# Moving the on-chip tiles of a hybrid encoder block so that their rows begin at multiples of 2 KB

## The chip, the core and the metric

The kernel runs on one core of a Trainium2 chip. The metric is device time in microseconds (us): the median of several executions. One more execution was recorded by the hardware profiler; its span is the time from the first to the last instruction of the program, and the execution's own time is a little longer than that.

The engines are TensorE (PE in the profile; PEld is its loading of the stationary operand), VectorE (DVE), ScalarE (ACT), GpSimd (POOL) and SyncE (SP). The on-chip memory has 128 partitions; a tile occupies the same byte range in each of them, and the tile's *offset* in this document is where that range begins. A matmul of this kernel reads two operands from it: the stationary one (128 columns of 4 bytes, 512 bytes per partition) and the moving one (256, 384 or 512 columns of 4 bytes).

## What is computed

One layer of an encoder block on 512 tokens of width 1024, all in float32:

```
xn   = rms_norm(h, g_mix);  proj = xn @ w_in          # 1024 -> 2048
h    = h + concat(short_conv(proj), pool(proj)) @ w_o # 1024 -> 1024
xn   = rms_norm(h, g_ffn);  q = xn @ w_q              # 1024 -> 2048
s    = q . sub_keys          # 8 heads x 2 halves x 128 keys
top-16 of each half -> 256 candidates -> top-16 experts of 16384, softmax
h    = h + sum_k gate_k * gelu(u_k . xn) * v_k
gate = sigmoid(rms_norm(h, g_ple) @ w_ple_gate)       # 1024 -> 1024
out  = rms_norm(h + gate * (p @ w_ple_proj), g_final)
```

## The kernel before

Every float32 product is made from three matmuls: an operand x is split into a high part H, which ScalarE writes as a copy in the reduced float32 format, and a low part L = x - H, which VectorE writes; then the kernel sums H·H, H·L and L·H (`mm3`, `mm3_pair`; lines 123, 125 and 127). A row of the profile such as `o<-vH,wL` names the output, then the moving operand, then the stationary one.

The stages follow each other along the span:

1. **Input projection** (from about 18 us): eight pieces of `w_in`, 256 columns each. `projT` multiplies a piece (stationary, `wH`/`wL`) with the transposed activations (moving, 512 columns, `xH`/`xL`). A piece is 48 matmuls.
2. **Output projection** (until about 160 us): the mixed activations `mixH`/`mixL` are stationary, the pieces of `w_o` (`wH`/`wL`, 256 columns) move.
3. **Query projection** (about 169 to 280 us): again `projT`, eight pieces of `w_q`; after each, 16 small matmuls with the keys give the scores, and VectorE begins the top-16 searches.
4. **First expert phase** (until about 640 us): for three of the four token groups, 384 tokens, all experts are evaluated densely, in blocks of 128. For each of the first 76 blocks `score` makes 24 matmuls: block `uH`/`uL` stationary, `xH`/`xL` moving with 384 columns. The blocks come by DMA into two buffers `uraw`; a load is issued when VectorE has made `uL` from the block before in that buffer. VectorE works through the top-16 searches meanwhile, and `onehot` spreads the gates with fp16 matmuls. The fourth token group gathers its experts row by row with indirect DMAs into `gr`.
5. **Second expert phase** (until about 1397 us): `mix` multiplies a block of `expert_v` (`vH`/`vL`, moving, 512 columns) with the weighted activations (`wH`/`wL` of the pool `wq`, stationary) into six accumulators `o`; the remaining 52 `score` blocks run in between, into `u`.
6. **Tail**: for each of the four token groups `tail_gate` multiplies the transposed activations `tH`/`tL` (stationary) with the gate weights. These lie in tiles that are free by then (`xH`/`xL` for the left 512 columns; `uraw`, `uH`, `uL` for the right 512) and move. The last group does its right half in two parts of 256 columns.

Memory is handed out by pools that grow from two ends. Pools without a side grow from the low end: the constants, then `xH`/`xL`, the `u` blocks, and in the second phase the `v` blocks and the pool `wq`. Pools with `side="right"` grow down from the high end: first `h`, then the weight pieces, `mixH`/`mixL`, scores, later `gr`, `gres`, the one-hot tiles and the tail's `tH`/`tL`. Tiles of a later stage take the place of those of an earlier one in the same stack.

The order of the instructions of the first four stages comes from a scheduler that runs when the program is built; the second expert phase and the tail stand in the order of the code.

Of the kernel before, what the change touches and what calls it, by code (L numbers as in the profile page):

```python
# [7 lines left out]
F32 = mybir.dt.float32  # L8
# [8 lines left out]
P = 128  # L17
# [43 lines left out]
def block_kernel(ctx: ExitStack, tc: tile.TileContext, x, pT_in, g_cols, w_in, conv_w, pool_w,  # L61
# [4 lines left out]
    consts = ctx.enter_context(tc.tile_pool(name="consts", bufs=1))  # L66
    dram = ctx.enter_context(tc.tile_pool(name="dram", bufs=1, space=bass.MemoryType.DRAM))
    small = ctx.enter_context(tc.tile_pool(name="small", bufs=2))
    sbx = ExitStack()
    xpool = sbx.enter_context(tc.tile_pool(name="xt", bufs=1))  # L70
    sh = ExitStack()
# [19 lines left out]
    eidx = consts.tile([P, P], I32, name="eidx")  # L91
    gate3 = consts.tile([P, P], F32, name="gate3")
    xrow = consts.tile([P, D], F32, name="xrow")

    def split_ld(src, hi, lo):
        nc.scalar.activation(hi, src, AF.Copy)
        nc.vector.tensor_tensor(lo, src, hi.bitcast(F32), op=OP.subtract)
# [900 lines left out]
```

## Time and profile before

| | before |
|---|---|
| median of 3 runs (lowest to highest) | 1455.18 us (1454.88 to 1456.47) |
| profiled execution, its own time | 1454.46 us |
| its span | 1452.7 us |
| mean granted TensorE clock | 0.994 of full speed |
| matmuls recorded | 7785 |

The profiled execution lies 0.72 us under the median and 1.8 us over its own span. TensorE's share of busy time in such a profile counts from the start of a matmul to its end, and matmuls overlap, so it shows whether TensorE waits and not how fast it goes; how fast it goes is the step from the start of one matmul to the start of the next, which the timeline gives.

### The profile page before, as it was taken

The page shows a single profiled execution, that of the slowest core. Times are in us where ns is not written, and L with a number is a line of the kernel's source. Part 1 is how long each engine was busy: PE and PEld are TensorE (multiplying, and loading weights), DVE is VectorE, ACT ScalarE, POOL GpSimd, SP SyncE. Part 2 cuts the span into 40 slices and gives each one's busy share as a digit, 9 for nine tenths or more (in the row PEclk, how much of TensorE's full clock was granted, in tenths as well). Part 3 has the DMA queues.
Part 4 walks back from the last instruction along what each step waited for, and adds up shares of the span by engine and source line. Part 5 has one row for each costly group of instructions (what it writes and reads, how often), then busy time and mean ns, then how long its engine had stood idle before and what let it go on. Part 6 is the DMA issues. An engine that isn't in the chain of part 4 may idle for free.

```text
span 1452.7 us, 20601 instructions
## 1 busy us (share of the span) xinstructions
PE 1430.8 (98%) x7785; PEld 1271.6 (88%) x7785; DVE 1137.7 (78%) x2078; ACT 614.5 (42%) x864; POOL 390.7 (27%) x260
## 2 busy tenths in 40 slices
PE   8999999999998999999999999999999999999997
PEld 5789888999998999998999999999998888788886
DVE  5644579899998987879988778888877777776765
ACT  5321533344564665664333333333333334433354
POOL 0000000002132132125766555454443123342000
PEclk9999999999998999999999999999999999999999
DMA  8223730047688899899998999998997899998721
GB/s 302 87 90 104 242 116 30 30 164 279 227 285 268 274 316 326 262 317 347 380 349 323 375 329 339 347 339 324 346 336 273 317 334 333 335 342 324 249 70 73
DMA packets 152083, 381.38 MB, mean 263 GB/s; under 512 B 10928, under 2 KB 72112, under 8 KB 151728
## 3 DMA queue, kind: packets, MB, share of 16 engines
q1 hardware_dynamic: 72400, 211.75, 41.3%
q0 software_dynamic: 36864, 134.23, 25.3%
q10 hardware_dynamic: 42720, 34.08, 7.2%
q8 instruction: 61, 1.00, 0.3%
q14 instruction: 38, 0.31, 0.1%
HBM read 339.92 MB, written 40.11 MB: 262 GB/s over the span
## 4 chain that ended last, share of the span: by engine, by line
PE 71%; DVE 12%; DMA 7%; issue 6%; ACT 2%; POOL 1%; ACTq 1%; SPq 0%; DVEq 0%; POOLq 0%
PE o L127 11%; PE o L123 11%; PE o L125 11%; PE acc L125 6%; PE acc L123 6%; PE acc L127 6%; PE u L127 5%; PE u L123 5%; PE u L125 5%; DMA uraw<-in_u_blk 3%; DVE uL L586 2%; DMA tH<-in_w_gate 2%; POOL gr L536 1%; PE acc L191 1%; PE tp L516 1%
## 5 line engine op out<-in xcount | busy, mean ns | idle before, releaser
L536 POOL DMA_INDIRECT gr<-in_u_rows,eidx x128 | 201.1, 1571 | 652.5 <-DVE tsm L390 334.6
L536 POOL DMA_INDIRECT gr<-in_v_rows,eidx x128 | 189.4, 1480 | 285.2 <-DVE xrow L560 274.5
L125 PE MATMUL o<-vL,wH 128*128 128x512 f32 x768 | 237.2, 390 | 0.7 <-DVE vL L604 0.7
L123 PE MATMUL o<-vH,wH 128*128 128x512 f32 x768 | 237.7, 390 | 0.3 <-ACT wH L685 0.3
L127 PE MATMUL o<-vH,wL 128*128 128x512 f32 x768 | 237.3, 390 | 0.1
L598 ACT ACTIVATE vH<-vraw 128x1024 fp32r<-128x1024 f32 x128 | 135.4, 1058 | 218.3 <-PE o L127 160.8
L123 PE MATMUL acc<-xH,uH 128*128 128x384 f32 x608 | 206.6, 340 | 3.4 <-ACT uH L580 3.4
L604 DVE TENSOR_TENSOR vL<-vraw,vH 128x1024 fp32r<-128x1024 f32 x128 | 156.2, 1221 | 65.2 <-ACT vH L598 64.9
L125 PE MATMUL acc<-xL,uH 128*128 128x384 f32 x608 | 206.8, 340 | 0.0
L127 PE MATMUL acc<-xH,uL 128*128 128x384 f32 x608 | 204.7, 339 | 0.2 <-DVE uL L586 0.2
L580 ACT ACTIVATE uH<-uraw 128x1024 fp32r<-128x1024 f32 x128 | 135.3, 1058 | 100.6 <-DMA uraw<-in_u_blk 64.0
L586 DVE TENSOR_TENSOR uL<-uraw,uH 128x1024 fp32r<-128x1024 f32 x128 | 155.7, 1217 | 24.8 <-ACT uH L580 24.8
L125 PEld LDWEIGHTS o<-vL,wH 128*128 128x128 f32 x768 | 144.0, 188 | 32.3 <-DVE vL L604 1.5
L127 PEld LDWEIGHTS o<-vH,wL 128*128 128x128 f32 x768 | 143.9, 188 | 31.2 <-DVE wL L690 1.0
L560 DVE SCALAR_TENSOR_TENSOR xrow<-gr,gate,xrow 128x1024 f32<-128x1024 f32 x128 | 164.1, 1282 | 5.1 <-DMA xrow<-h_d 4.6
L123 PEld LDWEIGHTS o<-vH,wH 128*128 128x128 f32 x768 | 143.3, 188 | 27.2 <-ACT wH L685 0.7
L556 DVE SCALAR_TENSOR_TENSOR gr<-gr,xrow 128x1024 f32<-128x1024 f32 x128 | 154.3, 1218 | 4.2 <-DMA gr<-in_u_rows,eidx 4.1
L127 PE MATMUL u<-xH,uL 128*128 128x384 f32 x416 | 139.6, 336 | 0.0
L123 PE MATMUL u<-xH,uH 128*128 128x384 f32 x416 | 139.5, 335 | 0.0
L125 PE MATMUL u<-xL,uH 128*128 128x384 f32 x416 | 139.3, 335 | 0.0
L123 PEld LDWEIGHTS acc<-xH,uH 128*128 128x128 f32 x608 | 115.4, 190 | 4.1 <-ACT uH L580 4.1
L127 PEld LDWEIGHTS acc<-xH,uL 128*128 128x128 f32 x608 | 115.1, 189 | 0.8 <-DVE uL L586 0.8
(214 smaller groups left out, 2336.8 us busy)
## 6 DMA issues: line engine op xcount, KB each, us to landing
uraw<-in_u_blk SPq DMA_DIRECT2D x128, 512.0 KB, 5.2
vraw<-in_v_rows SPq DMA_DIRECT2D x128, 512.0 KB, 6.0
G_d<-stage ACTq DMA_DIRECT2D x12, 1664.0 KB, 12.8
gq<-G_d SPq DMA_DIRECT2D x26, 768.0 KB, 7.0
A_d<-a ACTq DMA_DIRECT2D x17, 768.0 KB, 6.0
aq<-A_d SPq DMA_DIRECT2D x17, 768.0 KB, 9.5
wraw<-in_w_in SPq DMA_DIRECT2D x8, 1024.0 KB, 5.8
wraw<-in_w_q SPq DMA_DIRECT2D x8, 1024.0 KB, 5.8
```

Of the source, the lines that this page charges most:

```text
L123: nc.tensor.matmul(ps, lh, rh, start=start, stop=False)
L125: nc.tensor.matmul(ps, lh, rl, start=False, stop=False)
L127: nc.tensor.matmul(ps, ll, rh, start=False, stop=stop)
L191: nc.tensor.matmul(ps, pT[:, c, t * P:(t + 1) * P], wp[hf][:, c], start=c == 0, stop=c == 1)
L516: nc.tensor.matmul(ps[:, o:o + P], qb[b][:, t * P:(t + 1) * P], keys[:, 2 * hd + b], start=True, stop=True)
L536: nc.gpsimd.indirect_dma_start(out=g, out_offset=None, in_=table, in_offset=bass.IndirectOffsetOnAxis(ap=eidx[:, k:k + 1], axis=0))
L556: ins = nc.vector.scalar_tensor_tensor(g, g, 1.0, xrow, op0=OP.mult, op1=OP.mult, accum_out=act[:, k:k + 1])
L560: ins = nc.vector.scalar_tensor_tensor(accg, g, gate3[:, k - P:k - P + 1], accg, op0=OP.mult, op1=OP.add)
L580: nc.scalar.activation(ublk[i][1], ublk[i][0], AF.Copy)
L586: nc.vector.tensor_tensor(ublk[i][2], raw, uh.bitcast(F32), op=OP.subtract)
L598: nc.scalar.activation(vblk[n][1], vblk[n][0], AF.Copy)
L604: nc.vector.tensor_tensor(vblk[n][2], raw, vh.bitcast(F32), op=OP.subtract)
```

## The change

Two tiles are added that nothing reads or writes: 2016 bytes per partition as the first tile of the right side, and 256 bytes after the constants of the left side that are allocated first.

```diff
     small = ctx.enter_context(tc.tile_pool(name="small", bufs=2))
+    right = ctx.enter_context(tc.tile_pool(name="right", bufs=1, side="right"))
+    right.tile([P, 504], F32, name="rpad")
     sbx = ExitStack()
...
     xrow = consts.tile([P, D], F32, name="xrow")
+    consts.tile([P, 64], F32, name="lpad")
```

In the built program the offsets of the tiles move as follows (bytes per partition; in brackets the remainders by 2048 and by 64). Other buffers of a name lie whole multiples of 512 bytes further on.

| tile | side | before | with the change |
|---|---|---|---|
| `xH`, `xL` | left | 16128, 32512 (1792, 0) | 16384, 32768 (0, 0) |
| `uraw`, `uH`, `uL` | left | 48896, 57088, 69376 (1792, 0) | 49152, 57344, 69632 (0, 0) |
| `vH`, `vL` | left | 93952, 106240 (1792, 0) | 94208, 106496 (0, 0) |
| `wH`, `wL` of the second phase | left | 130816, 136960 (1792, 0) | 131072, 137216 (0, 0) |
| `wH`, `wL` of the projections | right | 180192, 196576 (2016, 32) | 178176, 194560 (0, 0) |
| `mixH`, `mixL` | right | 114656, 131040 (2016, 32) | 112640, 129024 (0, 0) |
| `tH`, `tL` of the tail | right | 176096, 184288 (2016, 32) | 174080, 182272 (0, 0) |
| `gr` | right | 204768 (2016, 32) | 202752 (0, 0) |
| `stage`, `a4` | right | 128992, 155616 (2016, 32) | 126976, 153600 (0, 0) |

No instruction is added, removed or moved on any engine. Only what three instructions of VectorE wait for changes, since other old and new tiles now share bytes: each of the `uL` below may only be written when the stores of `pleo` that lay there have landed. The first rows are VectorE's before, at the end of the transposition that precedes the query projection; the names in brackets are the semaphores waited for, where `DMAHW` stands for a DMA.

```order
153 L586 TENSOR_TENSOR uL<-uraw,uH 128x1024 [waits DMAHW4_49,Activation_49]
154 L139 SCALAR_TENSOR_TENSOR xL<-g,gcol,xH 128x512 [waits Activation_49]
155 L139 SCALAR_TENSOR_TENSOR xL<-tp,gcol,xH 128x512 [waits Activation_49]
156 L335 TENSOR_TENSOR xrow<-xs 128x1024 [waits DMAHW6_49,DVE_49]
157 L586 TENSOR_TENSOR uL<-uraw,uH 128x1024 [waits DMAHW3_49,DMAHW5_49,DMAHW2_49,Activation_49]
158 L586 TENSOR_TENSOR uL<-uraw,uH 128x1024 [waits DMAHW7_49,Activation_49]
159 L97 TENSOR_TENSOR wL<-wraw,wH 128x2048 [waits DMAHW1_49,PE_49,Activation_49]
160 L348 MAX tv<-s 128x8 [waits DMAHW0_49,Activation_49]
```

The same place with the change (line numbers are three higher there):

```order
153 L589 TENSOR_TENSOR uL<-uraw,uH 128x1024 [waits DMAHW7_49,DMAHW4_49,Activation_49]
154 L142 SCALAR_TENSOR_TENSOR xL<-g,gcol,xH 128x512 [waits Activation_49]
155 L142 SCALAR_TENSOR_TENSOR xL<-tp,gcol,xH 128x512 [waits Activation_49]
156 L338 TENSOR_TENSOR xrow<-xs 128x1024 [waits DMAHW6_49,DVE_49]
157 L589 TENSOR_TENSOR uL<-uraw,uH 128x1024 [waits DMAHW2_49,DMAHW5_49,DMAHW0_49,Activation_49]
158 L589 TENSOR_TENSOR uL<-uraw,uH 128x1024 [waits DMAHW7_49,DMAHW3_49,Activation_49]
159 L100 TENSOR_TENSOR wL<-wraw,wH 128x2048 [waits DMAHW1_49,PE_49,Activation_49]
160 L351 MAX tv<-s 128x8 [waits Activation_49]
```

The first, second and third `uL` wait for the first, the second and third, and the fourth of the last four `pleo` stores (line 193); before, it was the second `uL` (third and fourth store) and the `MAX` behind (second store). The instructions stand where they stood.

## Rows read from the trace of the kernel before

**Rows 1.** The page: the span, and busy us (share of the span) and instructions by engine.

```profile
span 1452.7 us, 20601 instructions
...
PE 1430.8 (98%) x7785; PEld 1271.6 (88%) x7785; DVE 1137.7 (78%) x2078; ACT 614.5 (42%) x864; POOL 390.7 (27%) x260
```

**Rows 2.** Groups by shape: line, engine, out<-in, shape, count | busy us, mean ns.

```profile
L123 PE MATMUL o<-vH,wH 128*128 128x512 f32 x768 | 237.7, 390 | 0.3 <-ACT wH L685 0.3
L123 PE MATMUL acc<-xH,uH 128*128 128x384 f32 x608 | 206.6, 340 | 3.4 <-ACT uH L580 3.4
L123 PE MATMUL u<-xH,uH 128*128 128x384 f32 x416 | 139.5, 335 | 0.0
L123 PE MATMUL acc<-xH,wH 128*128 128x512 f32 x256 | 83.3, 401 | 0.5 <-ACT xH L138 0.5
L123 PE MATMUL o<-xH,tH 128*128 128x512 f32 x32 | 12.9, 403 | 0.0
```

**Rows 3.** Timeline of PE, input projection: start us, us, instruction, count.

```profile
100.07 0.63 PE L123 MATMUL acc<-xH,wH 128*128 128x512 f32 x2
...
102.87 0.63 PE L123 MATMUL acc<-xH,wH 128*128 128x512 f32 x2
```

**Rows 4.** Timeline of PE, second expert phase, `mix`.

```profile
1289.91 0.62 PE L123 MATMUL o<-vH,wH 128*128 128x512 f32 x2
...
1295.35 0.62 PE L123 MATMUL o<-vH,wH 128*128 128x512 f32 x2
```

**Rows 5.** Timeline of PE, second expert phase, `score`.

```profile
702.79 0.33 PE L123 MATMUL u<-xH,uH 128*128 128x384 f32 x1
...
704.87 0.33 PE L123 MATMUL u<-xH,uH 128*128 128x384 f32 x1
```

**Rows 6.** Timeline of PE, output projection.

```profile
129.91 0.28 PE L123 MATMUL acc<-wH,mixH 128*128 128x256 f32 x1
...
131.47 0.28 PE L125 MATMUL acc<-wL,mixH 128*128 128x256 f32 x1
```

**Rows 7.** Timeline of PE, tail, last token group.

```profile
1438.95 0.28 PE L123 MATMUL o<-uraw,tH 128*128 128x256 f32 x1
...
1441.05 0.28 PE L123 MATMUL o<-uH,tH 128*128 128x256 f32 x1
```

**Rows 8.** DMA queues (packets, MB, share of 16 engines) over the whole span.

```profile
q1 hardware_dynamic: 72400, 211.75, 41.3%
q0 software_dynamic: 36864, 134.23, 25.3%
```

**Rows 9.** The longest of PE's waits between 40 and 640 us: total us, times, longest.

```profile
PE acc L123 <- ACT uH L580: 3.4, 3, 2.6
```

**Rows 10.** Windows: busy us and count by engine, PEclk, DMA share, GB/s.

```profile
190.00:240.00 50.00, 50.00 (x250) 41.56 (x249) 44.88 (x250) 16.34 (x20) 0.00 (x0) 1.00 0.28 85
240.00:280.00 40.00, 40.00 (x214) 34.51 (x213) 32.98 (x210) 10.11 (x16) 0.00 (x0) 1.00 0.00 1
280.00:440.00 160.00, 159.42 (x1031) 156.85 (x1031) 157.00 (x527) 85.42 (x128) 31.11 (x19) 1.00 0.68 229
450.00:460.00 10.00, 9.31 (x47) 8.87 (x48) 8.27 (x9) 5.06 (x11) 1.35 (x2) 0.66 1.03 329
460.00:470.00 10.00, 8.52 (x60) 7.67 (x59) 6.17 (x8) 6.06 (x11) 1.06 (x2) 0.85 0.56 189
```

**Rows 11.** Waits of VectorE between 190 and 280 us.

```profile
DVE tv L348 <- ACT s L518: 12.4, 5, 5.4
```

**Rows 12.** Timeline of ACT around 450 us; in brackets the idle time before and what ended it.

```profile
449.24 1.06 ACT L580 ACTIVATE uH<-uraw 128x1024 fp32r<-128x1024 f32 x1 [2.36 <-DMA uraw<-in_u_blk]
```

**Rows 13.** The stores of `pleo` (line 193): issues, first and last start; landing.

```profile
L193 SPq DMA_DIRECT2D ple_d<-pleo x8: 319/320/357, 13.8 to 168.7; - x8
...
DMA to landing us min/median/max: 5.8/7.2/8.4
```

**Rows 14.** Timeline of DVE: the first `uL`.

```profile
176.74 1.23 DVE L586 TENSOR_TENSOR uL<-uraw,uH 128x1024 fp32r<-128x1024 f32 x1 [0.99 <-ACT uH L580]
```

## The prediction

> **What bounds the kernel now.** I read the page first: TensorE is busy for 1430.8 of 1452.7 us [rows 1]. That says that it hardly waits, not that it is fast, since overlapping matmuls make "busy" blind to the distance between them. PE's waits come next: between 40 and 640 us, where DMA and VectorE are most in its way, the longest kind comes to 3.4 us in three times [rows 9]. So almost everywhere the time is the number of matmuls times the step from one start to the next, and the question is whether a tile's offset enters that step.
>
> The groups by shape raise the question by themselves. Matmuls of 512 columns last 390 ns on average in `mix`, but 401 in the projections and 403 in the tail [rows 2]. The timeline gives the steps; in each of these stretches PE runs without a wait:
>
> - `mix`, 512 columns: 24 matmuls from 1289.91 to 1295.35 us, 226.7 ns each [rows 4].
> - `score`, 384 columns: 12 from 702.79 to 704.87, 173.3 ns [rows 5].
> - Output projection, 256 columns: 13 from 129.91 to 131.47, 120.0 ns [rows 6].
> - Input projection, 512 columns: 12 from 100.07 to 102.87, 233.3 ns [rows 3].
> - Tail, 256 columns: 18 from 1438.95 to 1441.05, 116.7 ns [rows 7].
>
> From 384 to 512 columns (`score`, `mix`) the step grows by 53.4 ns, 0.417 ns a column, which is one column a cycle at the upper clock level of 2.4 GHz. Take 0.417 ns a column off each, and there remain 13.3 ns in `mix`, `score` and the output projection, 20.0 in the input projection and 10.0 in the tail's 256 columns. Two families, then. The table of offsets separates them: in the first three both operands lie on the same side, so their remainders by 64 are equal (0 and 0, or 32 and 32); in the last two the stationary operand lies on the right (32) and the moving one on the left (0). The strongest pair is output projection and tail: both take 256 columns, both run the same `mm3` chain into one bank, and their steps differ (120.0 and 116.7). Between them hardly anything but the operands' places is different.
>
> **What the change does, part by part.** No instruction moves; the pads cost no time.
>
> *Same-side matmuls* (`score`, `mix`, output projection): both operands move by the same number of bytes, so what they are to each other stays. The absolute remainder by 2048 does change, from 1792 or 2016 to 0. Does a moving row that crosses a multiple of 2 KB cost anything? In the output projection the moving rows of 1024 bytes begin at remainders 2016 and 992 in turn, so every second chunk of three matmuls crosses one and the next does not, and all 13 steps sum to 120.0 each [rows 6]. The stationary slices of `uH`, 512 bytes from remainder 1792 on, cross one in every fourth chunk; 12 steps over four chunks stay at 173.3 [rows 5]. So I take nothing here. The bound on the gain side is what exceeds 0.417 ns a column: 13.3 ns on 768 x 3 matmuls of `mix` and (608 + 416) x 3 of `score` [rows 2], 71 us. The bound on the loss side is that they fall into the slow family: 6.7 ns on 2304 of `mix`, 15 us.
>
> *Right-against-left matmuls* (both projections of 512 columns, the tail): afterwards both operands have remainder 0, as `mix` and `score` have now. If the remainder by 64 is what sorts the families, the step falls from 233.3 to 226.7. Their number is 256 x 3 = 768 `projT` matmuls [rows 2], of which half belong to each projection, and in the tail 32 x 3 = 96 for the left half [rows 2] plus three groups' right halves at 24 each, 168 together. 936 x 6.67 ns = 6.2 us. The last group's right half, 48 matmuls of 256 columns, would go the other way, from 116.7 to 120.0: 0.2 us lost. Sum: 6.1 us gained. From below: zero, if the offset isn't the reason.
>
> Does the gain reach the end? The first 2.6 us (input projection) do: PE paces that stage and all behind it shifts. The second 2.6 us (query projection) must also be taken up by VectorE, which has the top-16 searches there and is busy for 44.88 of 50 us from 190 to 240 and 157.00 of 160 from 280 to 440 [rows 10]. But from 240 to 280 it is busy for only 32.98 of 40 [rows 10], and in all it waits 12.4 us for the scores that PE feeds [rows 11]. It has caught up by then, so scores that come 2.6 us earlier let it go on earlier. If I am wrong there, these 2.6 us come back as waits of PE for `uL`, and the sum is 3.5 us. The tail's 0.9 us lies on the path to the last output.
>
> *DMA.* The gathers write to `gr`, remainder 32 by 64; most of the other loads write to `uraw` and `vraw`, remainder 0. Per engine the first queue moves 134.23 MB in 25.3% of 16 x 1452.7 us, 22.8 GB/s; the other 211.75 MB in 41.3%, 22.1 GB/s [rows 8]. The offset that is less round is not slower, so I take nothing. The bound for a gain is what PE loses around 450 us to a late load of `uraw`: 2.6 us of wait [rows 9, 12], and after it a granted clock of 0.66 over 10 us and 0.85 over the next [rows 10], about 9.8 us at the lower level, 1.2 GHz, worth 4.9 us: 7.5 us.
>
> *The three waits of VectorE.* The last `pleo` store is issued at 168.7 us and stores land within 8.4 us, by 177.1 [rows 13]; the first `uL` begins at 176.74 [rows 14] and waits for the first of the four, not the last. Nothing, then; without that cover, at most 0.4 us.
>
> Sum against the profiled execution: 1454.46 - 6.1 = 1448.4 us. The median lies 0.72 us above that execution, so the forecast for it is 1449.1 us.
>
> **A rule that speaks against this.** The Trainium skill, "TensorE: Matmul & The Clock Gate", section "Step-by-step: what each phase is for", says that PE reads the moving operand and the stationary one through two independent ports, so that loading the next tile's weights takes nothing from the running matmul. By that rule no offset of one to the other could matter, and the change would give 1455.2 us; the mechanism of the first rival below is this one. The same page's section "Back-to-back issue gap" gives N/2.4 + 2.5 ns for one matmul, 215.8 ns at 512 columns as an estimate; the trace agrees with neither family, at 226.7 and 233.3 [rows 3, 4].
>
> **The rivals.**
>
> *No change.* The families come from something that only coincides with the sides, such as the order in which stationary operands alternate: `projT` changes it with every matmul, `mix` keeps it for two. For it: five stretches are few. Against it: `score`, output projection and tail share one order of operands and fall into both families [rows 5 to 7]. Time: the median of before, 1455.2, give or take 1.2.
>
> *Half of it is swallowed.* The query projection's 2.6 us end at VectorE, as above: 1451.7 us.
>
> *Slower.* The place is the first expert phase around 450 us. There a `uraw` load is issued when VectorE is done with its predecessor, and PE already waited 2.6 us for one [rows 9, 12] and then fell to the lower clock [rows 10]. If PE comes 5.1 us earlier and neither VectorE nor the loads do, the 5.1 us turn into further waits, of which each of some 2.6 us brings a fall of the clock like the first one (0.66 over 10 us: 6.8 us at half speed, 3.4 us lost). Two more falls: 1455.2 - 6.1 + 5.1 + 6.8 = 1461.0. It decides from the point where waits and clock give back more than 9 us. Against it: VectorE waits for PE before this phase [rows 11], so both come earlier together.
>
> *More than forecast.* Rounder offsets make DMA quicker, the late load around 450 us is in time, and 7.5 us come on top: 1441.6. The rates of the two queues speak against it [rows 8]. The Trainium skill, "DMA: Bandwidth & Descriptors", section "How a descriptor splits into AXI transactions", has such a rule for reads that do not begin at a multiple of 256 bytes, which the stores from `stage` do not; by it this rival's time would be likelier. Nothing in the rows shows it, since a slower store and a slower load are not told apart there.
>
> **How the numbers follow.** Differences within 0.2%, 2.9 us, are about what a measurement here can't tell from no change. Forecast (6.1 us gained): 0.53. Swallowed half: 0.05. More: 0.04. These are faster: 0.62. No change: 0.29. Slower: 0.09. The likeliest case alone reaches from 1447.5 to 1451.7. The range takes in no change up to 1456.5 and leaves out the slower case, the larger gain and a remainder: 1446.5 to 1456.5.
>
> **What would show it.** Right: in the input projection the timeline steps by 226.7 ns, its group in the list by shape comes down from 401 to about 390 ns, that of the tail from 403 likewise; `mix`, `score` and the output projection keep 226.7, 173.3 and 120.0; the first expert phase begins about 5 us earlier, and the tail's 256 columns go to 120.0. The two queues keep their rates. Wrong: 233.3 ns in the projections at remainders of 0 refutes the step from remainders to families; 226.7 there with an unchanged end means that the gain was given back, and the clock and PE's waits from 400 to 470 us would show where; a changed step in `mix` or `score` would outweigh all else, at 2.3 us for each ns on `mix`.

## The result and the profile after

| | before | with the change |
|---|---|---|
| median (lowest to highest), 9 runs each | 1455.45 us (1452.8 to 1461.89) | 1448.09 us (1445.07 to 1450.09) |
| ratio, 95% interval | | 0.9941 (0.9929 to 0.9953) |
| profiled execution, its span | 1454.46, 1452.7 us | 1445.91, 1444.1 us |
| mean granted TensorE clock | 0.994 | 0.995 |

The change makes the kernel 7.4 us faster, and the interval does not reach "no change". The forecast was 1449.1 us.

The page shows the same matmuls, and TensorE busy for 7.2 us less than in [rows 1]; the DMA queues keep their shares, where [rows 8] had 41.3% and 25.3%.

```profile
span 1444.1 us, 20600 instructions
...
PE 1423.6 (99%) x7785; PEld 1272.1 (88%) x7785; DVE 1137.7 (79%) x2078; ACT 614.2 (43%) x864; POOL 383.2 (27%) x260
...
q1 hardware_dynamic: 72400, 211.75, 40.9%
q0 software_dynamic: 36864, 134.23, 25.4%
```

The groups by shape of the kernel after (busy us, mean ns behind the bar) show which matmuls changed. `mix` and both kinds of `score` keep the means of [rows 2], 390, 340 and 335 ns; the projections fall from 401 to 395 and the tail from 403 to 397.

```profile
L126 PE MATMUL o<-vH,wH 128*128 128x512 f32 x768 | 237.5, 390 | 0.0
...
L126 PE MATMUL acc<-xH,uH 128*128 128x384 f32 x608 | 206.6, 340 | 3.0 <-ACT uH L583 3.0
...
L126 PE MATMUL u<-xH,uH 128*128 128x384 f32 x416 | 139.5, 335 | 0.0
...
L126 PE MATMUL acc<-xH,wH 128*128 128x512 f32 x256 | 81.9, 395 | 0.5 <-ACT xH L141 0.5
...
L126 PE MATMUL o<-xH,tH 128*128 128x512 f32 x32 | 12.7, 397 | 0.0
```

The timeline of PE of the kernel after gives the steps, in the order input projection, output projection, `score`, `mix`, tail (256 columns).

```profile
100.00 0.62 PE L130 MATMUL acc<-xH,wL 128*128 128x512 f32 x2
...
102.72 0.62 PE L130 MATMUL acc<-xH,wL 128*128 128x512 f32 x2
...
126.81 0.28 PE L126 MATMUL acc<-wH,mixH 128*128 128x256 f32 x1
...
128.25 0.28 PE L126 MATMUL acc<-wH,mixH 128*128 128x256 f32 x1
...
696.79 0.33 PE L130 MATMUL u<-xH,uL 128*128 128x384 f32 x1
...
698.87 0.33 PE L130 MATMUL u<-xH,uL 128*128 128x384 f32 x1
...
1282.01 0.62 PE L130 MATMUL o<-vH,wL 128*128 128x512 f32 x2
...
1284.73 0.62 PE L130 MATMUL o<-vH,wL 128*128 128x512 f32 x2
...
1430.59 0.28 PE L126 MATMUL o<-uraw,tH 128*128 128x256 f32 x1
...
1432.75 0.28 PE L126 MATMUL o<-uH,tH 128*128 128x256 f32 x1
```

The input projection's 12 matmuls take 2.72 us, 226.7 ns each instead of 233.3 [rows 3]. Output projection (12 in 1.44 us, 120.0), `score` (12 in 2.08, 173.3) and `mix` (12 in 2.72, 226.7) stay as they were [rows 4 to 6]. The tail's 256 columns go from 116.7 [rows 7] to 120.0 (18 in 2.16).

To see where the time came from, follow the same six places in the timeline of PE: the first matmul of the input projection, its last pair, one of the last pairs of the query projection, the first `score` of the second phase, the first matmul of the tail and the last. In the kernel before (the line at 1265.30 us is a seventh, spoken of below):

```profile
18.84 0.47 PE L123 MATMUL acc<-xH,wH 128*128 128x512 f32 x1
...
113.60 0.63 PE L127 MATMUL acc<-xH,wL 128*128 128x512 f32 x2
...
272.39 0.63 PE L125 MATMUL acc<-xL,wH 128*128 128x512 f32 x2
...
651.89 0.33 PE L123 MATMUL u<-xH,uH 128*128 128x384 f32 x1
...
1265.30 0.74 PE L125 MATMUL o<-vL,wH 128*128 128x512 f32 x2 [0.72 <-DVE vL L604]
...
1397.95 0.48 PE L123 MATMUL o<-xH,tH 128*128 128x512 f32 x1
...
1444.43 0.28 PE L127 MATMUL u<-uH,tL 128*128 128x256 f32 x1
```

In the kernel after:

```profile
18.43 0.48 PE L126 MATMUL acc<-xH,wH 128*128 128x512 f32 x1
...
110.88 0.62 PE L130 MATMUL acc<-xH,wL 128*128 128x512 f32 x2
...
267.38 0.62 PE L128 MATMUL acc<-xL,wH 128*128 128x512 f32 x2
...
646.07 0.33 PE L126 MATMUL u<-xH,uH 128*128 128x384 f32 x1
...
1390.24 0.48 PE L126 MATMUL o<-xH,tH 128*128 128x512 f32 x1
...
1435.87 0.28 PE L130 MATMUL u<-uH,tL 128*128 128x256 f32 x1
```

The lead of the kernel after, by how much earlier the same matmul starts in it, grows from 0.41 to 2.72 us in the input projection, to 5.01 by the end of the query projection, to 5.82 by the second expert phase, to 7.71 by the tail and to 8.56 at its end. Three of these steps, 2.31 + 2.29 + 0.85 = 5.45 us, lie where the matmuls step faster. The other 3.1 us do not: 0.4 lie ahead of the first matmul, 0.8 come bit by bit in the first expert phase, and 1.9 come at one place, around 1265 us, where PE of this execution of before waits three times within 2.4 us (1.1 us in all, the longest for `vL`, the bracket at 1265.30), with longer steps in between, and in this one of after does not wait. Such waits differ between executions of one kernel: the change in its second profile (e11 below) waits there too, 0.7 us for `vL`, and spans 1445.9 us; e1 below, whose matmuls step as before, spans 1449.3, 3.4 us less than before. So the 3.1 us are no larger than what executions differ by, and nothing here puts them down to the change.

### The profile page after: what moved, and what is told of

It is laid out like the page before. It is cut to its first block, busy times and chain, and to the rows that moved or that the text cites. A ratio compares the mean times of both kernels' runs of the same rounds, so it can differ in the third digit from the quotient of the medians.

```text
span 1444.1 us, 20600 instructions
## 1 busy us (share of the span) xinstructions
PE 1423.6 (99%) x7785; PEld 1272.1 (88%) x7785; DVE 1137.7 (79%) x2078; ACT 614.2 (43%) x864; POOL 383.2 (27%) x260
## 4 chain that ended last, share of the span: by engine, by line
PE 79%; DVE 11%; DMA 6%; ACT 2%; issue 2%; ACTq 0%; SPq 0%; DVEq 0%
PE o L130 11%; PE o L126 11%; PE o L128 11%; PE acc L126 9%; PE acc L130 9%; PE acc L128 9%; PE u L130 5%; PE u L126 5%; PE u L128 5%; DMA uraw<-in_u_blk 3%; DMA tH<-in_w_gate 3%; DVE uL L589 2%; DVE vL L607 1%; PE g L473 1%; PE g L474 1%
## 5 line engine op out<-in xcount | busy, mean ns | idle before, releaser
L539 POOL DMA_INDIRECT gr<-in_v_rows,eidx x128 | 183.5, 1433 | 289.6 <-DVE xrow L563 278.9
L128 PEld LDWEIGHTS acc<-xL,uH 128*128 128x128 f32 x608 | 115.5, 190 | 0.0
```

The source lines that it names most:

```text
L128: nc.tensor.matmul(ps, lh, rl, start=False, stop=False)
L539: nc.gpsimd.indirect_dma_start(out=g, out_offset=None, in_=table, in_offset=bass.IndirectOffsetOnAxis(ap=eidx[:, k:k + 1], axis=0))
```

## The experiments

The offset that matters is called d here: the offset of the stationary tile minus that of the moving one, modulo 256. By the table of offsets the projections and the tail have d = 224 before and 0 after; `mix`, `score` and the output projection have d = 0 in both. All edits are in the two pads, or add another pad. Steps are read from the timeline, as above; where 227 stands it is the mean over both projections. Ratios are against the kernel before in the same batch.

| run | edit | median us, before | ratio (95%) | projection's d: step ns |
|---|---|---|---|---|
| e1_left_only | left pad alone | 1452.63, 1452.99 | 0.9995 (0.9975 to 1.0014) | 224: 233.3 |
| e2_right_only | right pad alone | 1447.23, 1452.99 | 0.9963 (0.9947 to 0.9979) | 0: 226.7 |
| e3_right_32b | right pad of 32 bytes alone | 1449.36, 1452.99 | 0.9973 (0.9959 to 0.9987) | 192: 229.2 |
| e4_left_32b | left pad of 32 bytes alone | 1451.89, 1452.99 | 1.0003 (0.9986 to 1.002) | 192: 229.2 |
| e5_swapped | left side at 32, right at 0 | 1458.22, 1453.35 | 1.0029 (1.0015 to 1.0044) | 224: 233.3 |
| e6_mix_apart | change, `mix` at d = 32 | 1464.46, 1453.35 | 1.0075 (1.0051 to 1.0099) | 0: 227 |
| e7_score_apart | change, `score` in both phases at d = 32 | 1450.43, 1453.35 | 0.9979 (0.9963 to 0.9996) | 0: 227 |
| e8_outproj_apart | change, output projection at d = 224 | 1447.7, 1453.35 | 0.9955 (0.9939 to 0.997) | 0: 227 |
| e9_both_apart | output projection and `score` at d = 224, projections equal | 1449.14, 1455.03 | 0.9961 (0.9944 to 0.9978) | 0: 227 |
| e10_apart_128 | the two sides 128 bytes apart | 1453.15, 1455.03 | 0.9985 (0.9966 to 1.0003) | 128: 233.3 |
| e11_change_again | the change once more | 1447.51, 1455.03 | 0.9943 (0.9923 to 0.9963) | 0: 226.7 |

### One pad alone

```diff
     xrow = consts.tile([P, D], F32, name="xrow")
+    consts.tile([P, 64], F32, name="lpad")
```

> Only the 256 bytes on the left: rows of the left tiles begin at multiples of 2 KB, the right stays at remainder 2016 (32 by 64). Theory A (the step depends on whether the two operands of a matmul have the same remainder by 64): nothing changes, projections 233.3 ns, tail 256 columns 116.7, mix 226.7, score 173.3; time as before, 1455 to 1456 us. Theory B (each operand gains where its rows begin at multiples of 2 KB): the moving operand of the projections is on the left, so part of the gain is here, 2 to 4 us, and mix and score, which lie wholly on the left, would gain too.

```diff
+    right = ctx.enter_context(tc.tile_pool(name="right", bufs=1, side="right"))
+    right.tile([P, 504], F32, name="rpad")
```

> Only the 2016 bytes on the right: the right at multiples of 2 KB, the left stays at remainder 1792 (0 by 64). Theory A: the whole gain, projections 226.7 ns, tail 226.7 and 120.0, time as with the full change, about 1448 us. Theory B: half of it at most, projections between 227 and 233 ns, about 1452 us.

The timeline of PE in the input projection, left pad alone (12 matmuls in 2.80 us, 233.3 ns):

```profile
99.63 0.63 PE L124 MATMUL acc<-xH,wH 128*128 128x512 f32 x2
...
102.43 0.63 PE L124 MATMUL acc<-xH,wH 128*128 128x512 f32 x2
```

The same, right pad alone (12 in 2.72, 226.7 ns):

```profile
99.65 0.61 PE L127 MATMUL acc<-xL,wH 128*128 128x512 f32 x2
...
102.37 0.61 PE L127 MATMUL acc<-xL,wH 128*128 128x512 f32 x2
```

The right pad does all of it and the left one nothing. With the right pad alone the left tiles stay at remainder 1792 of 2048, so rows that begin at multiples of 2 KB are not what helps; the left pad does bring `xH`, `uH` and `vH` to such multiples and gains nothing.

### Thirty-two bytes on either side

```diff
+    right = ctx.enter_context(tc.tile_pool(name="right", bufs=1, side="right"))
+    right.tile([P, 8], F32, name="rpad")
```

> 32 bytes on the right and nothing else: the right begins at remainder 1984 by 2 KB, 0 by 64; no tile's rows begin at a multiple of 2 KB. Theory A: the whole gain from 32 bytes, projections 226.7 ns, about 1448 us. Theory B: no gain, 233.3 ns, 1455 to 1456 us. If the remainder that counts were that by 128 or 256 (64 and 192 on the right here, 0 on the left), the steps would stay at 233.3 or take another value.

```diff
     xrow = consts.tile([P, D], F32, name="xrow")
+    consts.tile([P, 8], F32, name="lpad")
```

> 32 bytes on the left and nothing else: both sides then have remainder 32 by 64. Theory A (the two operands against each other): the whole gain, projections 226.7 ns, mix 226.7, score 173.3, about 1448 us. Theory C (each operand must itself begin at a multiple of 64): projections stay at 233.3 or get slower, and mix and score, which leave their multiples of 64, get slower too: at 6.7 ns on 2304 matmuls of mix alone 15 us, 1470 us or more.

```diff
+    right = ctx.enter_context(tc.tile_pool(name="right", bufs=1, side="right"))
+    right.tile([P, 504], F32, name="rpad")
...
     xrow = consts.tile([P, D], F32, name="xrow")
+    consts.tile([P, 72], F32, name="lpad")
```

> Right at remainder 0 by 64, left at 32: the change with 32 bytes more on the left, so that the two sides differ again, but with the stationary operand of the projections at the multiple of 64 and the moving one off it. If only the difference counts: 233.3 ns in the projections and the tail as before the change, about 1455 us. If it is the stationary operand's own remainder that counts: 226.7 ns, about 1448 us.

The timeline of PE in the input projection, e3_right_32b: 12 matmuls in 2.75 us, 229.2 ns, a value that neither family has.

```profile
99.80 0.62 PE L125 MATMUL acc<-xH,wH 128*128 128x512 f32 x2
...
102.55 0.62 PE L125 MATMUL acc<-xH,wH 128*128 128x512 f32 x2
```

e4_left_32b, where the two tiles lie elsewhere but as far apart by 256, has the same 229.2 (99.75 to 102.50 us), while its `mix`, whose tiles now both begin at 32 by 64, keeps 226.7 (12 matmuls from 1282.03 to 1284.75). In e5_swapped the sides change roles and d is again 224: 233.3, as before. So what counts is the difference of the two offsets, not where either begins. But remainders by 64 do not sort it: they are equal in e3 and e4, and the step is still 2.5 ns too long. By the step both should gain about 936 x 4.1 ns = 3.8 us: e3 did (0.27% of 1453 is 3.9), e4 did not; its interval goes from 2.0 us faster to 2.9 slower and leaves the 3.8 us out. The steps of e4 are clear, and why its median does not show them stays open: in the profiled executions e3 and e4 run alike and span 1448.3 and 1449.0 us, and no wait of PE accounts for more. e5 is slower than before for another reason, below.

### 128 bytes apart

```diff
+    right = ctx.enter_context(tc.tile_pool(name="right", bufs=1, side="right"))
+    right.tile([P, 472], F32, name="rpad")
...
     xrow = consts.tile([P, D], F32, name="xrow")
+    consts.tile([P, 64], F32, name="lpad")
```

> The change with 128 bytes less on the right: left at remainder 0, right at 128 by 256. If the period is 128 bytes: projections at 226.7 ns, as with the change. If it is 256: another step, between 226.7 and 233.3, perhaps the 229.2 of the kernels whose sides differ by 192. Time 1448 to 1450 us either way.

Timeline of PE, input projection, e10_apart_128 (12 in 2.80 us, 233.3 ns):

```profile
100.04 0.63 PE L128 MATMUL acc<-xL,wH 128*128 128x512 f32 x2
...
102.84 0.40 PE L128 MATMUL acc<-xL,wH 128*128 128x512 f32 x1
```

Both tiles are at multiples of 128 bytes and the step is the slow one. In e2 the two sides lie 256 apart by 2048 and the step is the quick one. So, if d alone decides, among powers of two 256 bytes is the period: 128 and all below it would make e10 quick, 512 and above would make e2 something else than the change. The time says the same, though weakly: e10's interval takes in no change, and its 1453.15 us missed the 1448 to 1450 that were expected either way.

### The other matmuls moved apart

```diff
     wq = vs.enter_context(tc.tile_pool(name="wq", reuse_waits="tile", bufs=2))
+    wq.tile([P, 8], F32, name="qpad", bufs=1)
```

> The change, and 32 bytes ahead of the tiles of the second phase's weighted activations: in mix alone the stationary operand has remainder 32 and the moving one 0. Theory A: mix steps by 233.3 instead of 226.7 ns, 2304 x 6.7 ns = 15.4 us more than the change, about 1463 us, with the projections still at 226.7. If the families of the projections came from the order of their operands and not from offsets: mix keeps 226.7, about 1448 us.

Timeline of PE, `mix`, e6_mix_apart: 12 in 2.80 us.

```profile
1299.88 0.63 PE L130 MATMUL o<-vH,wL 128*128 128x512 f32 x2
...
1302.68 0.63 PE L130 MATMUL o<-vH,wL 128*128 128x512 f32 x2
```

`mix`, which was quick before, steps by 233.3 ns in this stretch when its stationary tiles move by 32 bytes. Over all steps of `mix` the mean is 233.2 ns here and 227.6 in the kernel after, some of whose steps are longer than 226.7: 2304 x 5.6 = 12.9 us, where 15.4 were expected. A new wait of 3.6 us, told of below, and 3.4 us at the lower clock around it, worth 1.7, lie in it as well. The sum is 18.2 us; the profiled executions span 1461.3 and 1444.1 us, 17.2 apart, and the medians, of four executions here, are 16.4 apart (1464.46 to 1448.09). The steps are clear: the offsets alone make either family out of the same instructions.

```diff
     ub = sbx.enter_context(tc.tile_pool(name="ub", reuse_waits="tile", bufs=3))
+    ub.tile([P, 8], F32, name="upad", bufs=1)
```

> The change, and 32 bytes ahead of the tiles of the expert blocks: in score the stationary operand has remainder 32, the moving one 0; in mix both have 32; the tail's right half moves with 32 against 0. Theory A: mix stays at 226.7, projections at 226.7; score goes to another step. From 10.0 ns over the columns at 256 and 20.0 at 512, an estimate of 15 at 384: 175 ns, 3072 x 1.7 ns = 5 us more than the change, about 1453 us. If remainders of score's operands don't matter: 173.3 ns, about 1448 us.

```diff
     mixL = mpool.tile([P, DC, T], F32R, name="mixL")
+    mpool.tile([P, 8], F32, name="mpad")
```

> The change, and 32 bytes behind the mixed activations: in the output projection alone the stationary operand has remainder 32 and the moving one 0. Theory A, with the tail's 256 columns of before as the model: the step falls from 120.0 to 116.7 ns, 384 x 3.3 ns = 1.3 us less than the change, about 1446.8 us. If the tail's 116.7 came from something else: 120.0, about 1448 us.

Timeline of PE, output projection, e8_outproj_apart: 12 in 1.40 us, 116.7 ns.

```profile
126.97 0.28 PE L126 MATMUL acc<-wH,mixH 128*128 128x256 f32 x1
...
128.37 0.28 PE L126 MATMUL acc<-wH,mixH 128*128 128x256 f32 x1
```

At 256 columns apart is better, as in [rows 7]. The lead of e8 over the kernel before grows by 1.27 us across the output projection, 384 x 3.3 ns = 1.27. The medians, 1447.7 with it and 1448.09 and 1447.51 of the change, are too close to show that.

In e7_score_apart the 384 columns keep 173.3 ns at d = 32 (9 matmuls in 1.56 us, the last two lines), so the estimate of 175 was wrong. But ahead of them PE meets a wait that the change has not. The timeline of DVE and PE of e7_score_apart around 660 us, with `score` behind it:

```profile
659.94 0.96 DVE L694 TENSOR_TENSOR wL<-a,wH 128x768 fp32r<-128x768 f32 x1 [9.16 <-DMA G_d<-stage]
...
660.96 1.21 PE L130 MATMUL o<-vH,wL 128*128 128x512 f32 x2 [3.69 <-DVE wL L694]
...
696.87 0.34 PE L130 MATMUL u<-xH,uL 128*128 128x384 f32 x1
...
698.43 0.34 PE L130 MATMUL u<-xH,uL 128*128 128x384 f32 x1
```

The window behind the wait in e7_score_apart (busy us and count of PE, PEld, DVE, ACT and POOL, then PEclk, DMA share, GB/s):

```profile
660.00:670.00 10.00, 9.04 (x33) 7.37 (x34) 10.00 (x12) 1.91 (x2) 1.94 (x2) 0.83 0.59 199
```

The same window of the kernel after:

```profile
660.00:670.00 10.00, 10.00 (x46) 8.29 (x45) 10.00 (x14) 2.98 (x3) 5.54 (x4) 1.00 0.94 341
```

These read as one chain. In the change the first `wL` of the second phase ends at byte 140288, where a buffer of `stage` begins; the pad pushes its end 32 bytes into that buffer, whose store to `G_d` still runs. VectorE, idle for 9.16 us, waits last for that store, PE 3.69 us for VectorE, and then the granted clock is 0.83 where it is 1.00 in the change: 3.4 us at half speed, 1.7 us lost. The two together are 5.4 us; on the timeline e7 falls from 1.8 us behind the change to 7.3 across them. The same wait of PE for `wL` stands in e5_swapped, 4.1 us with 6.8 us of the lower clock from 660 to 670 us, and in e6_mix_apart, 3.6 us; their pads move that `wL` by the same 32 bytes, and in no other run here does PE wait for it so. That is why e5 is slower than before although none of its steps is.

Behind the wait e7 gains on the change: from 664 to 1087 us it makes up 2.8 of the 7.3 us. Over the whole second phase its `score` steps by 173.5 ns on average where the change has 174.4, because the slower steps after each `mix` are gone, and its `mix` by 226.8 where the change has 227.6. So in this profile 32 bytes between the operands of `score` pay, and the overlap takes back more than that. Wait, clock and this gain come to 2.6 us more than the change; the medians are 2.3 us apart (1450.43 and 1448.09), but e7 gains 4.5 us less on its own before (2.9 to 7.4), and its interval alone is 4.8 us wide, so the times do not test the sum. `score` at d = 32 without the overlap was not run.

### What is apart and pays, together

```diff
+    right = ctx.enter_context(tc.tile_pool(name="right", bufs=1, side="right"))
+    right.tile([P, 496], F32, name="rpad")
...
     xrow = consts.tile([P, D], F32, name="xrow")
+    consts.tile([P, 8], F32, name="lpad")
...
     mixL = mpool.tile([P, DC, T], F32R, name="mixL")
+    mpool.tile([P, 8], F32, name="mpad")
...
     ub = sbx.enter_context(tc.tile_pool(name="ub", reuse_waits="tile", bufs=3))
+    ub.tile([P, 56], F32, name="upad", bufs=1)
```

> Built from what the steps showed: the two sides at remainder 32 by 256 where the 512-column projections need equal remainders, but score and the output projection with operands 32 bytes apart, and mix with equal ones; no new tile overlaps one that is still being stored. Theory A as corrected (what counts is the difference of the two offsets): projections 226.7 ns, output projection 116.7, mix 226.7, and score with its slower steps after each mix gone, 173.3 on average instead of 174.4, which gives some 3 us from 655 to 1100 us. Sum against the change: 1.3 + 3 - 0.3 for the tail's right half, 4 us less, 1444 us beside 1448. If the gain of score was only that one run's: 1447.

Timeline of PE, `score`, e9_both_apart: from the first matmul to the `mix` matmul behind the sixth 1.06 us, 176.7 ns each.

```profile
696.82 0.34 PE L126 MATMUL u<-xH,uH 128*128 128x384 f32 x1
...
697.88 0.61 PE L126 MATMUL o<-vH,wH 128*128 128x512 f32 x2
```

Its pads keep `wL` clear of the `stage` buffer, and the wait of e7 is gone, as its cause would have it. But here `score` has d = 224 where e7 had 32, and it steps by 176.7 ns in every block that follows a `mix`: at 384 columns the sign can matter too. It does not always. In the same run, at the same d, the `score` matmuls ahead of the first `mix` step by 173.3 ns (18 in 3.12 us):

```profile
645.37 0.33 PE L126 MATMUL u<-xH,uH 128*128 128x384 f32 x1
...
648.49 0.33 PE L126 MATMUL u<-xH,uH 128*128 128x384 f32 x1
```

In the first expert phase both values occur (18 in 3.18 us from 559.70, 18 in 3.12 from 609.80). So d alone does not fix the step at 384 columns. What ran just before may have a part in it; no run here separates that.

The mean of `mix` comes down to 226.7 as in e7, and the output projection gains its 1.26 us on the timeline; the stretch from the first to the last `score` of the second phase is 0.7 us longer than in the change (452.7 to 452.0), and the tail, whose right half now has d = 32, 0.45 us longer. The kernel does not beat the change: 1449.14 us beside 1447.51 in the same batch, where 1444 or 1447 had been expected.

### The change again

> The change once more, beside the other two and the kernel before on the same chip, to compare with them: about 6 us less than before, 0.4%, with the steps that its first profile showed.

It measured 1447.51 us, 7.5 us less than before, with the steps of the change.

## Why the prediction was right

*The step paces the kernel, and the operands' places set the step.* Shown: 226.7 in the projections after, as forecast; the same instructions at 226.7, 229.2 or 233.3 ns by pads alone, and `mix` made slow by a pad of 32 bytes. The Trainium skill, "TensorE: Matmul & The Clock Gate", section "Step-by-step: what each phase is for", has the two operands read through independent ports, so that loading the next weights takes nothing from the running matmul. If that were all, the step could not depend on d; the runs at 512 columns do not agree (226.7 ns at d = 0, 229.2 at 192, 233.3 at 32, 128 and 224). The first rival, no change, rested on the same view and is out; its own example, the order of the stationary operands, is out by e6, which changes no order. The places are not the whole of it, though: in e9 one d gives two steps at 384 columns.

*Remainders by 64 sort the families.* Right for this change and wrong as a rule: e3 and e10 have equal remainders by 64 and step by 229.2 and 233.3. It is the difference by 256, which for this change gives the same forecast, since it goes from 224 to 0; that the pads chosen make both rules agree was luck. The five stretches that [rows 3 to 7] offered had differences of 0 and 224 only and could not tell the two rules apart.

*Crossing a multiple of 2 KB costs nothing.* Shown by e1 and e2, beside the unchanged 120.0, 173.3 and 226.7 after.

*The sum.* Forecast 2.6 + 2.6 + 0.9 = 6.1 us; on the timeline 2.31 + 2.29 + 0.85 = 5.45. The 226.7 ns hold for the stretch shown; over all of the two projections the steps average 227.2 ns after and 233.3 before, and 384 x 6.1 = 2.34 us is what each measured. That is the one term that was mis-sized, by 0.5 us in all. The last group's 256 columns did go to 120.0. The medians differ by 7.4 us (by the interval 6.8 to 10.3), and by 5.8 with the right pad alone (3.1 to 7.7). Whether the 1.4 us from 5.45 to the lower end of the first interval belong to the change stays open; e2, with the same steps, does not show them. The steps alone would bring the median to 1450.0 us, so that the forecast came within 1.0 us of 1448.09 is partly luck.

*The second 2.6 us pass VectorE.* Right: 5.01 us of lead at the end of the query projection and 5.82 at the second phase. VectorE's wait for the scores is there still, shorter (12.4 us in [rows 11]), in the waits of the kernel after between 190 and 280 us:

```profile
DVE tv L351 <- ACT s L521: 10.5, 5, 5.2
```

*DMA and the falls of the clock.* Right that nothing comes from the queues: their shares stand. PE's longest kind of wait between 40 and 640 us is still for `uH`, 3.0 us in 4 times with 1.3 the longest instead of 3.4 in 3 [rows 9]; and the ten microseconds of lower clock are still there, 5.4 us earlier, in the windows of the kernel after:

```profile
444.60:454.60 10.00, 9.50 (x47) 9.07 (x48) 8.27 (x9) 4.87 (x11) 1.48 (x1) 0.66 0.98 321
```

The granted clock there is 0.66, as in [rows 10]. So neither the rival "more", which needed this fall to vanish, nor "slower", which needed more of them, came about. What "slower" described did occur in the experiments, at another place: a wait of 3.7 us for `wL` and a lower clock behind it (e7).

*The three waits of VectorE.* Nothing to see: the `uL` that begins at 176.74 in [rows 14] begins in the timeline of DVE of the kernel after 3.0 us earlier, close to the 2.7 us of lead from the input projection, and what it waited for is still ScalarE.

```profile
173.75 1.23 DVE L589 TENSOR_TENSOR uL<-uraw,uH 128x1024 fp32r<-128x1024 f32 x1 [0.75 <-ACT uH L583]
```

## What to carry to other kernels

When TensorE hardly waits, compare the step from one matmul to the next between stretches of equal shape, not the share of busy time; a step that differs by a few per cent is a lead, and a table of the operands' offsets a cheap next look. Here stationary and moving tiles a multiple of 256 bytes apart were best at 512 columns, and one pad was enough; at 256 columns they were best apart, and at 384 one distance gave two steps, so measure the step in place. Before a pad is put in, look which tiles it pushes onto others that are still being stored: 32 bytes of overlap cost some 5 us here, more than the better place gained.

## What was not expected of the hardware

- The time between two matmuls depends on d in a way that changes with the columns: at 512 columns 226.7 ns at 0, 229.2 at 192, 233.3 at 32, 128 and 224; at 384 columns 173.3 at 0 and at 32, and at 224 either 173.3 or 176.7 for whole blocks (e9); at 256 columns 120.0 at 0 and 116.7 at 224, so that what is worst at 512 is best there. That the stationary operand's load meets the reads of the moving one in the memory is a guess that fits this; no run here shows the cause.
- Two tiles that share 32 bytes tie VectorE to the landing of another tile's store: 3.7 us of PE's time, and 3.4 us at the lower clock behind it (e7).
